# RWKV stage of a hybrid decoder step on one Trainium2 core: diagonal blocks stored to scratch by DMA from the product tile, five PSUM copies and an affine step on another engine

## The chip, the core and the metric

One core of one Trainium2 chip: TensorE (PE in the profile) with its weight loads (PEld), VectorE (DVE), ScalarE (ACT), GpSimd (POOL), the queue of SyncE (SP), from which all DMAs of this kernel are issued, and 16 DMA engines. The metric is the time of one execution in microseconds of the device.

## The reference

One layer over 1040 prompt tokens (16 of them meta tokens) and 8 x 8 sample tokens, everything in float32: a projection of the normed input to 5896 columns, an RWKV-7 branch and an mLSTM branch, a gated merge, and an MLP. The change touches the RWKV branch alone:

```python
a = jax.nn.sigmoid(a0 + al @ a_up)
w = -jax.nn.softplus(-(w0 + jnp.tanh(wl) @ w_up)) - 0.5        # decay = exp(-exp(w))
kk = heads(k * k_k); kk = kk * lax.rsqrt(jnp.maximum(jnp.sum(kk * kk, axis=-1, keepdims=True), 1e-24))
k = k * (1.0 + (a - 1.0) * k_a)

def _rwkv7_step(S, inp):
    r, w, k, v, kk, a = inp
    sa = jnp.einsum('bhvk,bhk->bhv', S, -kk)
    S = S * w[:, :, None, :] + sa[..., None] * (kk * a)[:, :, None, :] + v[..., None] * k[:, :, None, :]
    return S, jnp.einsum('bhvk,bhk->bhv', S, r)

y = _head_norm(y, gn_g, RW_GN_EPS) + gn_b
y = y + jnp.sum(r * k * r_k, axis=-1, keepdims=True) * v
y = y.reshape(B, T, D_RW) * g
```

There are 8 heads of 64. The scan over tokens is computed in chunks of 64 tokens, where the step above becomes matrix products and the inverse of a unit triangular 64x64 matrix.

## The kernel before

The RWKV part runs 24 passes: `j` counts 4 pairs of heads (two heads lie on the halves of the 128 partitions, `HP`), `g` counts 6 groups of `G` = 3 chunks; the last group (`g` = 5) also holds the 64 sample tokens. Each pass has four stages, written as generators that yield between their pieces: `stage_a` prepares the operands of a group and makes `X1`; `stage_b` of the group before inverts the triangular matrices; `stage_c` of the one before that carries the state; `stage_d` norms the output. `ORDER` says in which order the pieces of the four stages follow each other, and how many matmuls of the big input projection (`L283`, `L285`, `L287`) are pulled in between. The order on TensorE is thus written by hand and is kept as written. On VectorE, ScalarE, GpSimd and SP a scheduler places the instructions by its own estimate of when each can run, and each engine then executes its queue in order.

The names that matter here, with the lines of the profile:

- `X1` (`L713` on TensorE, `L715` on VectorE): three products per group, scaled and masked while they leave PSUM. Columns 128 to 192 of each chunk hold the strictly lower triangular matrix to be inverted.
- `nd4`, `nd` (`L719`, `L721`): `X1` masked to its four 16x16 blocks on the diagonal, and these folded to 16 columns. `nd` goes to scratch in DRAM (`ndr`, `L723`) and comes back as `NR` (`L725`), in which each partition holds a whole 16x16 block. Both are issued on SP, the second one when the first has landed.
- The chain on `NR` (`L773`, `L775`, tiles `tmp` and `x`): 15 rounds of a product and a sum on VectorE, which invert the 16x16 blocks. `XC` and `XT` (`L777`, `L780`) are the result and its transpose.
- The rest of `stage_b` widens the inverse from 16 to 32 to 64. TensorE makes products at `L785`, `L630`, `L801`, `L808` and `L814`, and between them their results leave PSUM: `QC`, `XC` again, `QZ` (`L803`, twice), the off-diagonal part of `bd["x"]` (`bdx`, `L810`, twice) and `ATb` (`L817` on ScalarE, `L818` on VectorE).
- `stage_c`: `L827` to `L831` multiply by `ATb`; `GH` and `MR` (`L838` to `L843`) leave PSUM; then, chunk after chunk, `L901` multiplies by the state `Vs` and `L909` on VectorE scales the new state out of PSUM. The next `L901` needs it.
- `stage_d`: squares (`sqd`), a sum over each head (`head_sum`, `L621` to `L623`, in which the part lost by a rounded copy is computed by the subtraction `L622` and added in a second matmul), a reciprocal root by Newton steps (`newton`, `L174` to `L182`), and `yo` (`L967` to `L969`).

Of the kernel before, what the change touches and what calls it, by code (L numbers as in the profile page):

```python
# [8 lines left out]
F32 = mybir.dt.float32  # L9
F32R = mybir.dt.float32r  # L10
I32 = mybir.dt.int32
AF = mybir.ActivationFunctionType
ALU = mybir.AluOpType
AX = mybir.AxisListType
# [15 lines left out]
G = 3  # L30
# [72 lines left out]
def tile_hybrid_trunk_step(ctx, tc, x_prompt, x_sample, st_S, st_shift, st_C, st_n, st_m, st_conv,  # L103
# [4 lines left out]
    nc = tc.nc  # L108
# [38 lines left out]
    dma = nc.sync.dma_start  # L147
    act = nc.scalar.activation
    V = nc.vector
# [225 lines left out]
    with banks(s=4, m=2), ExitStack() as st:  # L375
# [91 lines left out]
        with tc.manual_schedule(engines={mybir.EngineType.Activation, mybir.EngineType.PE}):  # L467
# [23 lines left out]
            V.tensor_scalar(out=NKK, in0=PRM[:, P_KK:P_KK + 4], scalar1=-1.0, scalar2=None, op0=ALU.mult)  # L491
            V.tensor_scalar(out=OKA, in0=PRM[:, P_KA:P_KA + 4], scalar1=-1.0, scalar2=1.0, op0=ALU.mult, op1=ALU.add)
            ps = sbank()
# [84 lines left out]
    ATb = gp.tile([128, G, 2, 2, 64], F32, name="ATb")  # L578
    KB = gp.tile([128, G, 3, 64], F32, name="KB")
    LMS = [gp.tile([128, G, 65], F32, name=f"LM{i}") for i in range(3)]  # L580
    for t_ in LMS:
# [23 lines left out]
    def g3(ap):  # L605
        return ap.rearrange("p (c t) -> p c t", c=G)
# [12 lines left out]
    def head_sum(ps, x, hi, lo, eng):  # L619
        hr, xr = hi.bitcast(F32R), lo.bitcast(F32R)  # L620
        nc.scalar.copy(out=hr, in_=x)  # L621
        eng.tensor_tensor(out=xr, in0=x, in1=hi, op=ALU.subtract)  # L622
        return lambda: [mm(ps(), lhsT=obr, rhs=t_, start=(y == 0), stop=(y == 1)) for y, t_ in enumerate((hr, xr))]  # L623

    def tl(n, sh=(GC,), bufs=1):
        return gp.tile([128] + list(sh), F32, tag=n, name=n, bufs=bufs)
# [15 lines left out]
    def stage_a(j, g, st):  # L642
# [34 lines left out]
        yield  # L677
        V.tensor_scalar(out=wa, in0=wa, scalar1=0.5, scalar2=0.5, op0=ALU.mult, op1=ALU.add)
        tw, ta = wa[:, 0], wa[:, 1]
        cc = tl("cc")  # L680
        V.tensor_tensor_scan(out=cc, data0=K["rms" if smp else "rm"], data1=tw, initial=0.0, op0=ALU.mult, op1=ALU.add)
# [11 lines left out]
        bt = tl("bt")  # L693
        V.scalar_tensor_tensor(out=bt, in0=zk, scalar=pc(P_KK), in1=ta, op0=ALU.mult, op1=ALU.mult)
        at = tw
        V.scalar_tensor_tensor(out=g3(at), in0=g3(zk), scalar=NKK[:, j:j + 1], in1=lx, op0=ALU.mult, op1=ALU.mult)
        for h, s in enumerate(HP):
            nc.scalar.copy(out=bd["a"][s, :, h, :], in_=g3(at)[s])
        V.tensor_tensor(out=KB[:, :, 2, :], in0=g3(bt), in1=g3(li), op=ALU.mult)
        act(out=ta, in_=ta, func=AF.Identity, scale=pc(P_KA), bias=OKA[:, j:j + 1])  # L700
        V.tensor_tensor(out=ta, in0=ta, in1=zk, op=ALU.mult)
# [15 lines left out]
        st["X1"] = X1  # L717
        nd4 = tl("bt", (G, 4, 16))
        V.tensor_tensor(out=nd4.rearrange("p c b s -> p c (b s)"), in0=X1[:, :, 128:192], in1=b3(K["m16"]), op=ALU.mult)  # L719
        nd = tl("nd", (G, 16))  # L720
        V.tensor_reduce(out=nd, in_=nd4.rearrange("p c b s -> p c s b"), axis=AX.X, op=ALU.add)  # L721
        scr = ndr[j * NG + g]
        dma(out=scr, in_=nd.rearrange("p c s -> p (c s)"))  # L723
        NR = tl("NR", (16, G, 16))
# [41 lines left out]
    def stage_b(j, g, st):  # L766
# [35 lines left out]
        for i, q in enumerate(HQ):  # L802
            V.tensor_copy(out=QZ[q], in_=ps[q, :32 * G])  # L803
        yield
# [4 lines left out]
        for h, q in enumerate(HQ):  # L809
            V.tensor_copy(out=bd["x"][q, :, h, 32:], in_=ps[q, :32 * G].rearrange("p (c d) -> p c d", c=G))  # L810
        yield
# [5 lines left out]
        nc.scalar.copy(out=at[HP[0], :, 0::3], in_=pv[HP[0]])  # L817
        V.tensor_copy(out=at[HP[1], :, 1:3], in_=pv[HP[1]])  # L818
        yield
# [123 lines left out]
    def stage_d(j, g, st):  # L943
# [11 lines left out]
        sv = sq[:, c0:].rearrange("p c t -> p (c t)")  # L955
        sr = head_sum(lambda: pv_[:, :ny], sv, tl("nt")[:, :ny], tl("yo")[:, :ny], PO)
        yield
# [904 lines left out]
```

## Time and profile before

| | us |
|---|---|
| three runs, median | 2055.19 |
| three runs, lowest and highest | 2053.84, 2058.42 |
| the profiled execution | 2053.6 |
| its span, from first to last instruction | 2051.8 |
| TensorE busy in the span | 1943.2 |
| VectorE busy in the span | 1266.4 |
| ScalarE busy in the span | 729.1 |
| GpSimd busy in the span | 589.4 |

The profile is of one execution. Busy times are unions of the instructions' times; matmuls overlap each other, so that a matmul row of 0.35 us may start 0.19 us behind the one before it. The RWKV passes run from about 95 to 830 us; the mLSTM branch, the merge and the MLP follow.

### The profile page before, as it was taken

The numbers are of one execution on the slowest core, as the hardware profiler recorded it, in microseconds if no ns is written. First come the engines' busy times: TensorE is split into PE (matmuls) and PEld (weight loads), VectorE is DVE, ScalarE is ACT, GpSimd is POOL, SyncE is SP. The second block draws the span as 40 slices with busy tenths as digits, with TensorE's granted clock in tenths as the row PEclk, the third lists the DMA queues.
The fourth block names the chain that finished last, engine by engine and source line by source line (L and its number), as shares of the span: only waits on it lengthen the run. The fifth ranks groups of instructions, "written<-read, shape, count | busy, mean of one in ns | idle before, by whom it ended". The sixth has DMA issues, their size and how long they took to land.

```text
span 2051.8 us, 32757 instructions
## 1 busy us (share of the span) xinstructions
PE 1943.2 (95%) x12325; PEld 1762.7 (86%) x12325; DVE 1266.4 (62%) x3527; ACT 729.1 (36%) x1706; POOL 589.4 (29%) x937
## 2 busy tenths in 40 slices
PE   8999899999999999999899998999999999999996
PEld 8988788888888888989788777889999999988895
DVE  6378778867877887777765469244444444444447
ACT  6444344433443343546554234322222222211122
POOL 3321221322122121353435115133222322232225
PEclk9999999999999999999999999999999999999998
DMA  5222112112111221143756334111111111111114
GB/s 157 56 77 66 47 56 64 58 47 67 63 56 56 67 66 57 54 129 117 233 185 206 132 99 153 32 52 42 52 52 42 42 51 43 42 42 52 42 37 163
DMA packets 148495, 161.63 MB, mean 79 GB/s; under 512 B 20428, under 2 KB 121606, under 8 KB 148336
## 3 DMA queue, kind: packets, MB, share of 16 engines
q1 hardware_dynamic: 148336, 159.54, 24.6%
q8 instruction: 97, 1.59, 0.3%
q14 instruction: 62, 0.51, 0.1%
HBM read 121.98 MB, written 37.27 MB: 78 GB/s over the span
## 4 chain that ended last, share of the span: by engine, by line
PE 63%; DVE 22%; DMA 7%; issue 3%; ACT 2%; POOL 1%; SPq 0%; DVEq 0%; ACTq 0%; POOLq 0%
PE g L219 11%; PE g L221 11%; PE g L220 11%; PE g L287 5%; PE g L283 5%; PE g L285 5%; DMA NR<-ndr 3%; DVE tmp L773 2%; DVE x L775 2%; DMA ndr<-nd 1%; PE g L1735 1%; DVE Vs L909 1%; PE a L713 1%; PE g L1635 1%; PE g L1637 1%
## 5 line engine op out<-in xcount | busy, mean ns | idle before, releaser
L207 POOL TENSOR_TENSOR lo<-raw,hi 128x128 fp32r<-128x128 f32 (+1 forms) x736 | 414.7, 596 | 985.8 <-ACT hi L200 971.6
L283 PE MATMUL g<-u,hi 128*128 128x414 f32 (+4 forms) x1120 | 379.8, 339 | 1.5 <-ACT hi L200 0.8
L287 PE MATMUL g<-u,lo 128*128 128x414 f32 (+4 forms) x1120 | 381.0, 340 | 0.0
L285 PE MATMUL g<-u,hi 128*128 128x414 f32 (+4 forms) x1120 | 378.9, 338 | 0.0
L200 ACT CAST hi<-raw 128x1024 fp32r<-128x1024 f32 x124 | 128.6, 1048 | 379.3 <-PE g L1735 275.8
L219 PE MATMUL g<-mg,hi 128*128 128x384 f32 (+1 forms) x768 | 251.7, 328 | 0.6 <-ACT mg L1609 0.6
L220 PE MATMUL g<-mg,hi 128*128 128x384 f32 (+1 forms) x768 | 251.4, 327 | 0.3 <-DVE mg L1610 0.3
L221 PE MATMUL g<-mg,lo 128*128 128x384 f32 (+1 forms) x768 | 251.5, 328 | 0.0
L1771 DVE TENSOR_TENSOR ACC<-g,ACC 128x512 f32<-128x512 f32 x234 | 161.4, 690 | 129.5 <-PE g L221 123.4
L283 PEld LDWEIGHTS g<-u,hi 128*128 128x128 f32 x1120 | 214.1, 191 | 6.8 <-issue 1.5
L287 PEld LDWEIGHTS g<-u,lo 128*128 128x128 f32 x1120 | 213.8, 191 | 4.9 <-POOL lo L207 0.3
L285 PEld LDWEIGHTS g<-u,hi 128*128 128x128 f32 x1120 | 213.7, 191 | 3.7 <-issue 0.2
L219 PE MATMUL g<-hi,ah 128*128 128x512 f32 (+1 forms) x515 | 202.9, 394 | 0.0
L220 PE MATMUL g<-lo,ah 128*128 128x512 f32 (+1 forms) x515 | 202.7, 394 | 0.0
L221 PE MATMUL g<-hi,ah 128*128 128x512 f32 (+1 forms) x515 | 202.4, 393 | 0.0
L219 PEld LDWEIGHTS g<-mg,hi 128*128 128x128 f32 x768 | 144.1, 188 | 1.5 <-ACT mg L1609 0.9
L220 PEld LDWEIGHTS g<-mg,hi 128*128 128x128 f32 x768 | 144.2, 188 | 1.2 <-DVE mg L1610 0.5
L221 PEld LDWEIGHTS g<-mg,lo 128*128 128x128 f32 x768 | 144.2, 188 | 0.0
L221 PEld LDWEIGHTS g<-hi,ah 128*128 128x128 f32 x515 | 96.7, 188 | 22.9
L219 PEld LDWEIGHTS g<-hi,ah 128*128 128x128 f32 x515 | 96.6, 187 | 22.3
L220 PEld LDWEIGHTS g<-lo,ah 128*128 128x128 f32 x515 | 96.7, 188 | 22.0
L773 DVE TENSOR_TENSOR tmp<-NR,x 128x45 f32<-128x45 f32 (+4 forms) x360 | 82.5, 229 | 28.4 <-DMA NR<-ndr 21.1
(855 smaller groups left out, 3482.1 us busy)
## 6 DMA issues: line engine op xcount, KB each, us to landing
raw<-in_w_in_dram SPq DMA_DIRECT2D x44, 512.0 KB
raw<-in_w_ff_up_dram SPq DMA_DIRECT2D x32, 512.0 KB
raw<-in_w_ff_down_dram SPq DMA_DIRECT2D x32, 512.0 KB
NR<-ndr SPq DMA_DIRECT2D x24, 384.0 KB
gscr<-gst SPq DMA_DIRECT2D x16, 544.0 KB
xt<-in_x_prompt_dram SPq DMA_DIRECT2D x15, 512.0 KB
ga<-gscr SPq DMA_DIRECT2D x8, 544.0 KB
pscr<-ga SPq DMA_DIRECT2D x8, 544.0 KB
```

Of the source, the lines that this page charges most:

```text
L200: nc.scalar.copy(out=hi, in_=raw)
L207: PO.tensor_tensor(out=lo[:, k:k + step], in0=raw[:, k:k + step], in1=hi[:, k:k + step].bitcast(F32), op=ALU.subtract)
L219: mm(ps, lhsT=wh, rhs=xh, start=(i == 0), stop=False)
L220: mm(ps, lhsT=wh, rhs=xl, start=False, stop=False)
L221: mm(ps, lhsT=wl, rhs=xh, start=False, stop=(i == last))
L283: mm(ps, lhsT=hi[:, k], rhs=xh, start=(k == 0), stop=False)
L285: mm(ps, lhsT=hi[:, k], rhs=xl, start=False, stop=False)
L287: mm(ps, lhsT=lo[:, k], rhs=xh, start=False, stop=(k == 7))
L713: mm(ps[:, 192 * (c - c0):192 * (c - c0) + 192], lhsT=flat(bd["a"][:, c]), rhs=flat(KB[:, c]), start=True, stop=True)
L773: V.tensor_tensor(out=tmp[:, :, :n], in0=NR[:, s + 1:16, :, s].rearrange("p t c -> p c t"), in1=x[:, :, s:s + 1].broadcast_to([128, G, n]) ...
L775: V.tensor_tensor(out=x[:, :, s + 1:16], in0=x[:, :, s + 1:16], in1=tmp[:, :, :n], op=ALU.add)
L1771: V.tensor_tensor(out=ACC[:, i, cs], in0=ps, in1=ACC[:, i, cs], op=ALU.add)
```

## The change

The diagonal blocks go from `X1` to scratch by eight DMAs, one for each 16 partitions (16 partitions x 3 chunks x 16 numbers); `nd4`, `nd` and their two instructions are gone. The two `QZ` copies, the two `bdx` copies and the second half of `ATb` are issued on ScalarE. The step from tanh to sigmoid is no longer one VectorE instruction over both halves of `wa`: the `w` half is done on ScalarE, and for the `a` half 0.5 is folded into the constants (`OKA`, `PRH`) and 1.0 is added in `bt`; the factor `k_k` moves into the second `KB` product. The subtraction in `head_sum` for `sqd` runs on VectorE, where GpSimd had it.

```diff
-            V.tensor_scalar(out=OKA, in0=PRM[:, P_KA:P_KA + 4], scalar1=-1.0, scalar2=1.0, op0=ALU.mult, op1=ALU.add)
+            V.tensor_scalar(out=OKA, in0=PRM[:, P_KA:P_KA + 4], scalar1=-0.5, scalar2=1.0, op0=ALU.mult, op1=ALU.add)
...
-        V.tensor_scalar(out=wa, in0=wa, scalar1=0.5, scalar2=0.5, op0=ALU.mult, op1=ALU.add)
         tw, ta = wa[:, 0], wa[:, 1]
+        act(out=tw, in_=tw, func=AF.Identity, scale=0.5, bias=half)
...
-        V.scalar_tensor_tensor(out=bt, in0=zk, scalar=pc(P_KK), in1=ta, op0=ALU.mult, op1=ALU.mult)
+        V.scalar_tensor_tensor(out=bt, in0=ta, scalar=1.0, in1=zk, op0=ALU.add, op1=ALU.mult)
...
-        V.tensor_tensor(out=KB[:, :, 2, :], in0=g3(bt), in1=g3(li), op=ALU.mult)
-        act(out=ta, in_=ta, func=AF.Identity, scale=pc(P_KA), bias=OKA[:, j:j + 1])
+        V.scalar_tensor_tensor(out=KB[:, :, 2, :], in0=g3(bt), scalar=PRH[:, P_KK + j:P_KK + j + 1], in1=g3(li), op0=ALU.mult, op1=ALU.mult)
+        act(out=ta, in_=ta, func=AF.Identity, scale=PRH[:, P_KA + j:P_KA + j + 1], bias=OKA[:, j:j + 1])
...
-        nd4 = tl("bt", (G, 4, 16))
-        V.tensor_tensor(out=nd4.rearrange("p c b s -> p c (b s)"), in0=X1[:, :, 128:192], in1=b3(K["m16"]), op=ALU.mult)
-        nd = tl("nd", (G, 16))
-        V.tensor_reduce(out=nd, in_=nd4.rearrange("p c b s -> p c s b"), axis=AX.X, op=ALU.add)
         scr = ndr[j * NG + g]
-        dma(out=scr, in_=nd.rearrange("p c s -> p (c s)"))
+        for r in range(0, 128, 16):
+            dma(out=scr[r:r + 16].rearrange("p (c s) -> p c s", c=G), in_=X1[r:r + 16, :, 128 + r % 64:144 + r % 64])
...
-            V.tensor_copy(out=QZ[q], in_=ps[q, :32 * G])
+            nc.scalar.copy(out=QZ[q], in_=ps[q, :32 * G])
...
-            V.tensor_copy(out=bd["x"][q, :, h, 32:], in_=ps[q, :32 * G].rearrange("p (c d) -> p c d", c=G))
+            nc.scalar.copy(out=bd["x"][q, :, h, 32:], in_=ps[q, :32 * G].rearrange("p (c d) -> p c d", c=G))
...
-        V.tensor_copy(out=at[HP[1], :, 1:3], in_=pv[HP[1]])
+        nc.scalar.copy(out=at[HP[1], :, 1:3], in_=pv[HP[1]])
...
-        sr = head_sum(lambda: pv_[:, :ny], sv, tl("nt")[:, :ny], tl("yo")[:, :ny], PO)
+        sr = head_sum(lambda: pv_[:, :ny], sv, tl("nt")[:, :ny], tl("yo")[:, :ny], V)
```

The order on TensorE is the same in both programs, and on SP the eight DMAs stand where the one stood, with `NR` right behind them. The scheduler's order on VectorE changes. Three places show it; lines of the changed program are one or two off those of before (`L772` and `L774` are the chain).

On VectorE in the pass `j` = 2, `g` = 2, from the row ahead of the chain's first product on (`128x3x15`), before:

```order
L174 SCALAR_TENSOR_TENSOR nt<-nt 128x192
L773 TENSOR_TENSOR tmp<-NR,x 128x3x15
L174 SCALAR_TENSOR_TENSOR dg<-nt,dg 128x192
L818 COPY ATb<-b 64x3x128
L967 SCALAR_TENSOR_TENSOR yo<-ys,PRM,dg 128x192
L775 TENSOR_TENSOR x<-x,tmp 128x3x15
L968 SCALAR_TENSOR_TENSOR yo<-yo,PRM,bv 128x192
L773 TENSOR_TENSOR tmp<-NR,x 128x3x14
L756 TENSOR_TENSOR bv<-a,Zv 128x192
L969 TENSOR_TENSOR yo<-yo,gg 128x192
L775 TENSOR_TENSOR x<-x,tmp 128x3x14
L838 TENSOR_TENSOR GH<-s,Ct 64x3x64 x2
```

The same stretch in the changed program, up to the first round of the chain:

```order
L636 TENSOR_TENSOR MB<-a,Ct 128x3x64
L174 SCALAR_TENSOR_TENSOR nt<-nt 128x192
L174 SCALAR_TENSOR_TENSOR dg<-nt,dg 128x192
L966 SCALAR_TENSOR_TENSOR yo<-ys,PRM,dg 128x192
L967 SCALAR_TENSOR_TENSOR yo<-yo,PRM,bv 128x192
L968 TENSOR_TENSOR yo<-yo,gg 128x192
L755 TENSOR_TENSOR bv<-a,Zv 128x192
L837 TENSOR_TENSOR GH<-s,Ct 64x3x64 x2
L841 TENSOR_TENSOR MR<-s,RB_764 64x3x64 x2
L772 TENSOR_TENSOR tmp<-NR,x 128x3x15
L774 TENSOR_TENSOR x<-x,tmp 128x3x15
```

`dg`, the three `yo`, `bv`, `GH` and the first `MR` pair now stand ahead of the chain, where they stood behind its first product; `ATb` is gone from the queue.

On VectorE in a pass with sample tokens (`j` = 2, `g` = 5), around the same product, before:

```order
L803 COPY QZ<-b 32x96 x2
L773 TENSOR_TENSOR tmp<-NR,x 128x3x15
L775 TENSOR_TENSOR x<-x,tmp 128x3x15
L961 TENSOR_SCALAR sqd<-c 128x192
L773 TENSOR_TENSOR tmp<-NR,x 128x3x14
L176 TENSOR_SCALAR dg<-sqd 128x192
L775 TENSOR_TENSOR x<-x,tmp 128x3x14
L174 SCALAR_TENSOR_TENSOR nt<-dg 128x192
L810 COPY bdx<-b 32x3x32 x2
L179 TENSOR_TENSOR nt<-nt,sqd 128x192
L773 TENSOR_TENSOR tmp<-NR,x 128x3x13
L174 SCALAR_TENSOR_TENSOR dg<-nt,dg 128x192
```

and in the changed program:

```order
L793 STREAM_TRANSPOSE XT<-XC 128x192
L960 TENSOR_SCALAR sqd<-c 128x192
L176 TENSOR_SCALAR dg<-sqd 128x192
L174 SCALAR_TENSOR_TENSOR nt<-dg 128x192
L179 TENSOR_TENSOR nt<-nt,sqd 128x192
L174 SCALAR_TENSOR_TENSOR dg<-nt,dg 128x192
L174 SCALAR_TENSOR_TENSOR nt<-dg 128x192
L182 TENSOR_TENSOR nt<-nt,sqd 128x192
L772 TENSOR_TENSOR tmp<-NR,x 128x3x15
L174 SCALAR_TENSOR_TENSOR nt<-nt 128x192
L774 TENSOR_TENSOR x<-x,tmp 128x3x15
L174 SCALAR_TENSOR_TENSOR dg<-nt,dg 128x192
```

The rows from `sqd` to the fourth Newton product (seven rows) have moved ahead of the chain's first product, and the `QZ` and `bdx` copies are gone.

On VectorE in the pass behind it (`j` = 3, `g` = 0), from the chain's first product on, before; the first pair of `Vs` rows is the fifth row after the last one shown:

```order
L773 TENSOR_TENSOR tmp<-NR,x 128x3x15
L775 TENSOR_TENSOR x<-x,tmp 128x3x15
L773 TENSOR_TENSOR tmp<-NR,x 128x3x14
L843 TENSOR_TENSOR MR<-s,Ct 64x2x64 x2
L775 TENSOR_TENSOR x<-x,tmp 128x3x14
L663 TENSOR_SCALAR rho<-a 64x2
L848 TENSOR_TENSOR mq<-s,Ct 128x64
L664 TENSOR_SCALAR rho<-a 64x1
L663 TENSOR_SCALAR rho<-a 64x2
L664 TENSOR_SCALAR rho<-a 64x1
L773 TENSOR_TENSOR tmp<-NR,x 128x3x13
L665 RECIPROCAL rho<-rho 128x3
```

and in the changed program, up to that pair:

```order
L842 TENSOR_TENSOR MR<-s,Ct 64x2x64 x2
L665 TENSOR_SCALAR rho<-a 64x2
L847 TENSOR_TENSOR mq<-s,Ct 128x64
L666 TENSOR_SCALAR rho<-a 64x1
L665 TENSOR_SCALAR rho<-a 64x2
L666 TENSOR_SCALAR rho<-a 64x1
L667 RECIPROCAL rho<-rho 128x3
L772 TENSOR_TENSOR tmp<-NR,x 128x3x15
L774 TENSOR_TENSOR x<-x,tmp 128x3x15
L772 TENSOR_TENSOR tmp<-NR,x 128x3x14
L774 TENSOR_TENSOR x<-x,tmp 128x3x14
L908 TENSOR_SCALAR Vs<-c,LM_759 64x65 x2
```

The second `MR` pair, `rho` and `mq` have moved ahead of the chain, and `Vs` follows after two rounds instead of four and a half.

## Rows read from the trace of the kernel before

**Rows 1.** The page, its first part: the span, and the busy time of TensorE with its share of the span and its instructions.

```profile
span 2051.8 us, 32757 instructions
...
PE 1943.2 (95%) x12325; PEld 1762.7 (86%) x12325; DVE 1266.4 (62%) x3527; ACT 729.1 (36%) x1706; POOL 589.4 (29%) x937
```

**Rows 2.** Busy time of each engine (us, and instructions) in two stretches, 95 to 830 us and the rest to the end, with the granted clock, the DMA share and GB/s.

```profile
95.00:830.00 735.00, 679.74 (x5462) 622.33 (x5461) 570.01 (x2120) 292.35 (x795) 158.32 (x322) 0.98 0.20 60
830.00:2051.00 1221.00, 1174.87 (x6303) 1055.59 (x6301) 647.43 (x1295) 382.55 (x796) 396.08 (x534) 0.99 0.27 87
```

**Rows 3.** The waits of 95 to 830 us: engine and line that waited, what it waited for, us in total, times, longest us.

```profile
PE c L901 <- DVE Vs L909: 39.3, 38, 2.8
...
DVE tmp L773 <- DMA NR<-ndr: 21.1, 11, 4.2
...
PE b L814 <- DVE bdx L810: 4.6, 3, 1.7
```

**Rows 4.** TensorE in order of time in one pass, 510.5 to 537 us: start, us, engine, line, operation, written tile <- read tiles, form, count; in brackets the idle time before it and what ended that.

```profile
511.10 0.54 PE L785 MATMUL b<-XC,X 64*64 64x32 f32 x12
...
517.78 0.83 PE L814 MATMUL b<-X,bdx 128*128 128x128 f32 x6
...
520.72 0.83 PE L827 MATMUL s<-MB,ATb 128*128 128x128 f32 x6
...
529.21 0.34 PE L901 MATMUL c<-Vs,GH 128*64 128x65 f32 x4 [1.71 <-DVE Vs L909]
...
532.71 0.34 PE L901 MATMUL c<-Vs,GH 128*64 128x65 f32 x4 [0.61 <-DVE Vs L909]
...
536.44 0.54 PE L785 MATMUL b<-XC,X 64*64 64x32 f32 x12
```

**Rows 5.** VectorE in the same pass, the same columns.

```profile
510.89 1.07 DVE L715 SCALAR_TENSOR_TENSOR X<-a,rho,Ct 128x192 f32<-128x192 f32 x3 [1.71 <-PE a L713]
...
512.42 0.49 DVE L721 TENSOR_REDUCE nd<-bt 128x48 f32<-128x192 f32 x1
...
514.80 0.51 DVE L803 COPY QZ<-b 32x96 f32<-32x96 f32 x2 [0.47 <-PE b L801]
...
519.42 0.23 DVE L773 TENSOR_TENSOR tmp<-NR,x 128x45 f32<-128x45 f32 x1
519.57 0.34 DVE L174 SCALAR_TENSOR_TENSOR dg<-nt,dg 128x192 f32<-128x192 f32 x1
519.95 0.56 DVE L818 COPY ATb<-b 64x384 f32<-64x384 f32 x1
520.54 0.42 DVE L967 SCALAR_TENSOR_TENSOR yo<-ys,PRM,dg 128x192 f32<-128x192 f32 x1
...
521.26 0.64 DVE L968 SCALAR_TENSOR_TENSOR yo<-yo,PRM,bv 128x192 f32<-128x192 f32 x1
...
522.31 0.36 DVE L756 TENSOR_TENSOR bv<-a,Zv 128x192 f32<-128x192 f32 x1
522.58 0.35 DVE L969 TENSOR_TENSOR yo<-yo,gg 128x192 f32<-128x192 f32 x1
...
523.23 0.73 DVE L838 TENSOR_TENSOR GH<-s,Ct 64x192 f32<-64x192 f32 x2
524.00 0.72 DVE L842 TENSOR_TENSOR MR<-s,RB 64x192 f32<-64x192 f32 x2
...
529.30 0.35 DVE L678 TENSOR_SCALAR wa<-wa 128x384 f32<-128x384 f32 x1
...
535.59 0.36 DVE L777 TENSOR_TENSOR XC<-x,Ct 128x192 f32<-128x192 f32 x1
```

**Rows 6.** The SP queue in order of time in two stretches, 206 to 209 us and 512.8 to 515.2 us: start, us for which the queue is held (where there is a count, for all of them), line, written <- read.

```profile
206.54 1.13 SPq L518 DMA_DIRECT2D wur<-in_rw_w_up_dram  x2
207.71 1.24 SPq L518 DMA_DIRECT2D wur<-in_rw_a_up_dram  x2
...
512.93 0.32 SPq L723 DMA_DIRECT2D ndr<-nd  x1
514.45 0.61 SPq L725 DMA_DIRECT2D NR<-ndr  x1
```

**Rows 7.** Groups of instructions by line and form in 95 to 830 us: line, engine, operation, written <- read, form, count, then busy us and mean ns of one, then idle time before them and what ended it.

```profile
L810 DVE COPY bdx<-b 32x96 f32<-32x96 f32 x48 | 11.9, 249 | 2.7 <-PE b L808 1.7 <-issue 0.2
...
L817 ACT COPY ATb<-b 64x384 f32<-64x384 f32 x24 | 11.3, 472 | 7.9 <-PE b L814 7.8
L622 POOL TENSOR_TENSOR yo<-sqd,nt 128x192 fp32r<-128x192 f32 x19 | 11.3, 595 | 26.9 <-ACT nt L621 14.4 <-DMA yscr<-yo 7.0 <-DVE X L715 3.1
...
L739 ACT COPY Vs<-a 64x65 f32<-64x65 f32 x48 | 9.9, 207 | 0.6
...
L719 DVE TENSOR_TENSOR bt<-X,Ct 128x192 f32<-128x192 f32 x24 | 9.0, 373 | 0.1
```

**Rows 8.** The chain that ended last, in order of time, 408 to 419 us: start, us, what.

```profile
407.70 1.07 DVE X L715 x3
...
409.78 3.42 DMA ndr<-nd
...
413.22 5.40 DMA NR<-ndr
...
418.65 0.24 DVE tmp L773
```

More of the change, by code (lines that the diff above doesn't have):

```diff
@@ L579, in tile_hybrid_trunk_step @@
     KB = gp.tile([128, G, 3, 64], F32, name="KB")
+    half = gp.tile([128, 1], F32, name="half")
+    V.memset(half, 0.5)
     LMS = [gp.tile([128, G, 65], F32, name=f"LM{i}") for i in range(3)]
```

## The prediction

> **What bounds the kernel now.** The page comes first: TensorE is busy 95% of the span and carries most of the chain that ended last [rows 1]. So an edit on VectorE can only give back time in which TensorE stands still. The windows say where that is: the RWKV part, 95 to 830 us, holds 735 - 680 = 55 us of idle TensorE and a VectorE that is busy 570 us of 735; behind it the touched code no longer runs [rows 2]. 55 us, 2.7%, is the ceiling. The waits then say what TensorE stands still for: 39 us for `Vs`, the scaled PSUM evacuation on VectorE, in 38 waits of up to 2.8 us, and 4.6 us for `bdx`; VectorE in turn waits 21 us, in 11 of 24 passes, for `NR`, which comes back through DRAM [rows 3].
>
> To see what ends last, walk one pass (j = 2, g = 2, 511 to 536 us) on both engines. TensorE starts `L785` at 511.10 and again at 536.44: the period is 25.34 us. It reaches `L827` at 520.72, 9.62 us later, without a wait; its idle time, 1.71 + 0.61, comes behind that, at the two `Vs` waits [rows 4]. VectorE makes `X1` at 510.89 to 511.96, first uses `NR` at 519.42, starts `GH` at 523.23, about 1.6 us after `L827` has made it possible (520.72 + 0.83 of matmuls = 521.6 at the earliest), and ends with `XC` at 535.59, on which the next `L785` rests [rows 4, 5]. From `GH` on, VectorE runs almost back to back. It is late there, `Vs` sits in the same queue, and so TensorE waits.
>
> **What the change takes and adds, per pass.** VectorE loses the mask product and the reduction (0.37 + 0.49), four small copies (4 x 0.25), the large copy (0.56) and the affine step (0.35) [rows 5, 7]: 2.8 us. It gains the subtraction, 0.36 as the `bv` row, a plain product of the same 128x192, has it [rows 5]; a scalar added to the second `KB` product is below 0.1. Net about -2.4 us in each of 24 passes, 57 us in all if every one of them lay on the path.
>
> ScalarE gains the copies: a 64x65 copy takes 0.21 there and the sister copy of `ATb` 0.47 [rows 7], so 4 x 0.22 + 0.47 + some 0.36 = 1.7 us per pass. It is busy 292 of 735 us [rows 2], so I price this at nothing. The cover is thin at one place: `L814` at 517.78 needs `bdx` [rows 4], and on ScalarE four `Vs` copies now stand ahead of it. Without the cover it costs up to 0.3 us a pass, 7 us in all, on the stretch to `L827`. GpSimd loses 0.6 us [rows 7] for which nobody waits.
>
> **The transfer.** Before, `NR`'s second transfer is issued at 514.45, that is 2.49 us after `X1` ends: 0.97 for mask and reduction, then 1.52 from issue to landing of one DMA, of which the issue holds the queue 0.32 [rows 5, 6]. Now eight DMAs must be issued one after the other, and all must land. Their issue price is in no row. Below: 0.32 each, as the one they replace. Above: the four `wur` loads, also of a part of the partitions, take 1.13 + 1.24 = 2.37 us, 0.60 each, and `NR`'s own issue 0.61 [rows 6]. I take 0.60, since these transfers are like those pieces of a tensor rather than a whole one. Then the last issue ends 8 x 0.60 = 4.8 us after `X1`, it lands as long after its issue as before (1.52 - 0.32 = 1.2, say 1.2 to 1.5), and `NR` is issued at 6.0 to 6.3 instead of 2.49: 3.6 later. By the low price it would be 8 x 0.32 + 1.2 = 3.8, 1.3 later. With 5.0 for `NR` itself (514.45 to 519.42 [rows 5, 6]) the first `tmp` can start 11.2 us after `X1`, where it was 7.5.
>
> The Trainium skill, page "DMA: Bandwidth & Descriptors", Specifications, asks for at least 512 bytes per piece, below which the engine does a read-modify-write; the new pieces have 64. The old ones had 192 and the whole transfer was through in 1.52 us [rows 6], so no such penalty shows in the rows; doubling a transfer of this size would move the sum by some tenths of a microsecond at most, and I leave it out.
>
> **Where the pass then ends.** The order of the instructions, the first pair of order rows above, decides it: in the new program `GH` and `MR` stand ahead of the first `tmp`. So `tmp` starts at the later of two times, counted from `L785`. By `NR`: `X1` ends at 0.86 and `NR` is there at 0.86 + 11.2 = 12.1. By `GH`: `L827` at 9.62, `GH` at 10.5, `GH` and `MR` 1.45: 12.0. They meet, which is why I see no large gain and no large loss here. What remains behind `tmp` was 16.17 us (519.42 to 535.59). Of it go, to ScalarE or ahead of the wait, `dg` 0.34, `ATb` 0.56, three `yo` (0.42, 0.64, 0.35), `bv` 0.36, `GH` 0.73, `MR` 0.72 and the affine step 0.35: 4.5 us; the subtraction's 0.36 comes [rows 5]. That leaves 12.1. With `XC`'s 0.36 and 0.1 to the matmul the period is 12.1 + 12.1 + 0.5 = 24.7 against 25.34: 0.6 us. The `Vs` waits shrink by about 1.5 us, but a wait of `L785` for `XC` takes most of their place.
>
> Named by `j` and `g`, seven passes are of this kind (g = 2 and 3, but for the very first): 7 x 0.6 = 4.2 us. Three long ones (g = 5, j < 3) have the scratch transfer stuck, behind a weight load: 3.42 us, and `tmp` 9.9 us after `X1` [rows 8]. There the eight issues run while the first one waits anyway, so `NR` comes 1.9 later (4.8 + 1.5 + 5.4 = 11.7); but behind `tmp` two `bdx` copies and `ATb` (1.1) go, seven rows of the Newton steps (about 2.4, at 0.35 each) move ahead of the wait, and 0.36 comes: -3.1. Gain 1.2 each, 3.5 us together; TensorE's wait for `bdx` [rows 3], which was queued behind this wait, goes with it. The three passes after them (g = 0, j > 0) have `Vs` close behind the `NR` wait, the 2.8 us of [rows 3]: `NR` comes 2 to 3.6 later, but five rows of the chain, one `MR` pair and six short rows no longer stand between (some 0.22, 0.6 and 0.17 each, as such rows take): -2.7. About 0. In six passes (g = 4 and g = 1, without first and last) a long run of matmuls lies behind `XC`, and only their `Vs` wait shortens, by 0.25 as I estimate from the two limits: 1.5 us. The first two and the last two passes, where less leaves the tail, lose 1 together by the same two limits (an estimate). Sum: 4.2 + 3.5 + 0 + 1.5 - 1 = 8 us. The profiled execution took 2053.6, so 2045.6 by its own account; it was 1.6 below the median of the three runs, 2055.19, which gives **2047 us**.
>
> **Rivals.** (1) *All of the relief arrives*: issues at 0.32, `NR` 2.3 earlier than I take it, and a tail 0.6 shorter than its rows add up to. Then the seven gain 1.2 each, the long three 2.5, the three after them 1.3, the six 1.0: 8.4 + 7.5 + 3.9 + 6 + 1 = 27, half of the 55 us: 2028. For it: VectorE runs back to back when TensorE waits [rows 4, 5]. Against: two limits meet at 12 us, and the issue price moves only one of them. (2) *`NR` is late* (slower). Each microsecond beyond 11.2 costs that much in the some 17 passes in which `tmp` waits for `NR`: 8/17 = 0.5 us eats the gain, that is an issue price of 0.66; at 0.75 per issue, or a landing 1.2 us longer, it is 17 x 1.2 - 8 = 12 us slower: 2067. For it: `NR`'s own issue at 0.61, and the queue also carries the weight loads. Against: four issues in 2.37 us. (3) *The eight pay one by one*: each issue waits for the landing before it, 8 x 1.52 = 12.2 us before `NR` can be issued, 9.7 later than now, of which some 5 us reach the period: 24 x 5 = 120 us, 2175. The `wur` rows speak against it, with four issues in 2.4 us [rows 6]. The Trainium skill, page "DMA: Bandwidth & Descriptors", Rules for kernel authors, says of two transfers to disjoint partition halves that they serialize and that splitting is not worth it; by that rule the time would go this way. (4) *ScalarE's copies stand in the way*: 0.3 to 0.5 us in each pass before `L827`, which eats the 8 us: no change. (5) *Nothing moves*, since removed waits only change their name: 2055.
>
> **How the numbers follow.** A measurement here tells 0.2%, 4 us. Chances: forecast, 2040 to 2051, 35%; rival 1, 14%; rivals 4 and 5, 22%; rival 2, 26%; rival 3, 3%. Faster is the first two, 49%; same 22%; slower 29%. The range takes in most of rivals 1 and 2: 2028 to 2069.
>
> **What would show it.** SP: eight issues per pass, 0.6 apart (0.32: rival 1). `tmp` about 11 us behind `X1`, with waits for `NR` in more passes than 11, together some 30 us instead of 21. TensorE's waits for `Vs` down from 39 to below 20 us, new ones of `L785` for `XC`, about 1 us each. VectorE some 57 us less busy, ScalarE 40 us more, TensorE's idle time in 95 to 830 us at 47. Waits of `L808`, `L814` or `L827` for ScalarE would be rival 4. The prediction is wrong if the eight issues cost other than 0.5 to 0.66 each, or if VectorE stands idle behind `tmp`.

## The result and the profile after

The changed kernel takes **2082.2 us** (median of four runs, 2079.0 to 2084.2) where the kernel before, run beside it, takes 2056.8: a ratio of 1.0119, 95% interval 1.0092 to 1.0146. It is 25 us slower; 8 us faster had been forecast, and the range ended at 2069. The profiled execution took 2083.5. The page, first the span and then busy time and share of each engine:

```profile
span 2081.7 us, 32856 instructions
PE 1963.2 (94%) x12325; PEld 1782.0 (86%) x12325; DVE 1206.7 (58%) x3360; ACT 773.7 (37%) x1850; POOL 570.6 (27%) x913
```

The work moved as intended: VectorE is 60 us less busy than before, ScalarE 45 us more. But TensorE, with the same 12325 instructions in the same order, is busy 1963.2 us instead of 1943.2 [rows 1]: the same matmuls ran slower. The windows of the RWKV part and of what follows (length, busy time and instructions of each engine, the granted clock, the share and the rate of the DMA engines):

```profile
95.00:860.00 765.00, 700.00 (x5464) 641.86 (x5463) 507.70 (x1950) 337.01 (x938) 144.56 (x302) 0.95 0.21 58
860.00:2081.00 1221.00, 1174.25 (x6294) 1054.95 (x6292) 649.58 (x1296) 382.24 (x796) 391.03 (x529) 0.99 0.27 87
```

The second row has the 1221 us that the stretch behind the RWKV part had before [rows 2]; the 30 us lie in the first, and its clock fell from 0.98 to 0.95. Two accounts say how much each is. TensorE's idle time is the span less its busy time: 2051.8 - 1943.2 = 108.6 before, 118.5 now, 10 us more. Time lost to the clock is the span by what is missing of the mean granted clock, 0.987 before and 0.975 now: 26.7 and 52.0, 25 us more. (Together 35 for 30, since part of a slow stretch can lie in idle time.) These are two single executions, and the one of the kernel before had a higher clock than most: over 80 executions of that kernel the clock loss averages 34.4 us, and over the four of the changed kernel 49.4 us, which makes 15 of the 24 us between their mean times. **So by either account most of the loss is a slower TensorE, and the waits themselves are the smaller part.**

The waits of the same stretch (total, times, longest, in us) against [rows 3]:

```profile
DVE tmp L772 <- DMA NR<-ndr: 51.9, 24, 3.8
PE c L900 <- DVE Vs L908: 46.4, 35, 3.8
PE b L784 <- DVE XC L776: 10.8, 10, 5.5
```

All 24 passes now wait for `NR`, TensorE's waits for `Vs` grew instead of shrinking, and the longest single ones are 3.8 and 5.5 us, where 2.8 was the longest for `Vs`. What one does is seen in the pass j = 1, g = 0, first on VectorE, then on TensorE (start, duration, shape, in brackets idle time before and who ended it):

```profile
286.51 0.18 DVE L667 RECIPROCAL rho<-rho 128x3 f32<-128x3 f32 x1
290.29 0.23 DVE L772 TENSOR_TENSOR tmp<-NR,x 128x45 f32<-128x45 f32 x1 [3.61 <-DMA NR<-ndr]
...
291.17 0.58 DVE L908 TENSOR_SCALAR Vs<-c,LM 64x65 f32<-64x65 f32 x2
```

```profile
287.75 0.34 PE L285 MATMUL g<-u,hi 128*128 128x398 f32 x1
291.80 0.49 PE L900 MATMUL c<-Vs,GH 128*64 128x65 f32 x4 [3.72 <-DVE Vs L908]
...
292.93 0.53 PE L283 MATMUL g<-u,hi 128*128 128x398 f32 x1
```

```profile
284.00:288.00 4.00, 4.00 (x28) 3.59 (x27) 1.86 (x10) 2.26 (x7) 3.21 (x8) 1.00 0.46 122
288.00:291.80 3.80, 0.09 (x1) 0.00 (x0) 1.36 (x7) 0.00 (x0) 0.00 (x0) 0.94 0.85 244
291.80:305.00 13.20, 13.20 (x56) 11.74 (x56) 6.73 (x30) 4.45 (x12) 1.16 (x2) 0.50 0.02 6
305.00:309.00 4.00, 4.00 (x32) 3.70 (x33) 3.50 (x15) 0.00 (x0) 0.62 (x1) 1.00 0.15 33
```

VectorE has nothing left that stands ahead of `tmp` and waits 3.61 us. `Vs`, whose matmul has long been done, stands four rows behind `tmp` in the same queue, so TensorE waits 3.72 us for it. Behind the wait the granted clock is 0.50, that is 1.2 GHz, for all 13.2 us that the third window shows, with TensorE busy all the time and a matmul on 398 columns at 0.53 us. Half of 13.2 is lost on top of the wait. Along the whole RWKV part the trace has 72 us at 1.2 GHz, 24 before; 13 of the 17 TensorE waits of 1.5 us or more have such a stretch beginning in them or within 2 us behind them. This is no rule: in the kernel before it holds for 2 of 8 such waits, and in the run e1 below for 2 of 10.

### The profile page after: what moved, and what is told of

It reads as the page before. It is cut to its first block, busy times and chain, and to the rows that moved or that the text cites. A ratio compares the mean times of both kernels' runs of the same rounds, so it can differ in the third digit from the quotient of the medians.

```text
span 2081.7 us, 32856 instructions
## 1 busy us (share of the span) xinstructions
PE 1963.2 (94%) x12325; PEld 1782.0 (86%) x12325; DVE 1206.7 (58%) x3360; ACT 773.7 (37%) x1850; POOL 570.6 (27%) x913
## 5 line engine op out<-in xcount | busy, mean ns | idle before, releaser
L207 POOL TENSOR_TENSOR lo<-raw,hi 128x128 fp32r<-128x128 f32 (+1 forms) x736 | 409.9, 592 | 1045.4 <-ACT hi L200 1028.1
L287 PE MATMUL g<-u,lo 128*128 128x414 f32 (+4 forms) x1120 | 387.2, 346 | 0.0
L283 PE MATMUL g<-u,hi 128*128 128x414 f32 (+4 forms) x1120 | 385.9, 345 | 0.8 <-ACT hi L200 0.8
L285 PE MATMUL g<-u,hi 128*128 128x414 f32 (+4 forms) x1120 | 384.4, 343 | 0.0
L283 PEld LDWEIGHTS g<-u,hi 128*128 128x128 f32 x1120 | 218.6, 195 | 6.2 <-issue 1.5
L287 PEld LDWEIGHTS g<-u,lo 128*128 128x128 f32 x1120 | 218.0, 195 | 5.4 <-POOL lo L207 0.3
L285 PEld LDWEIGHTS g<-u,hi 128*128 128x128 f32 x1120 | 218.4, 195 | 4.0 <-issue 0.2
L219 PEld LDWEIGHTS g<-hi,ah 128*128 128x128 f32 x515 | 96.6, 187 | 22.3
L772 DVE TENSOR_TENSOR tmp<-NR,x 128x45 f32<-128x45 f32 (+4 forms) x360 | 74.5, 207 | 59.6 <-DMA NR<-ndr 51.9
```

The source lines that it names most:

```text
L207: PO.tensor_tensor(out=lo[:, k:k + step], in0=raw[:, k:k + step], in1=hi[:, k:k + step].bitcast(F32), op=ALU.subtract)
L219: mm(ps, lhsT=wh, rhs=xh, start=(i == 0), stop=False)
L283: mm(ps, lhsT=hi[:, k], rhs=xh, start=(k == 0), stop=False)
L285: mm(ps, lhsT=hi[:, k], rhs=xl, start=False, stop=False)
L287: mm(ps, lhsT=lo[:, k], rhs=xh, start=False, stop=(k == 7))
L772: V.tensor_tensor(out=tmp[:, :, :n], in0=NR[:, s + 1:16, :, s].rearrange("p t c -> p c t"), in1=x[:, :, s:s + 1].broadcast_to([128, G, n]) ...
```

## The experiments

All times are medians; idle and clock loss come from each profiled execution as above, and the last column is the clock loss as the mean over all executions of a kernel, since one execution can lie far from it (e6 was profiled in its slowest execution, e17 in its fastest). The first `tmp` is given as its start less the end of `X1`, mean of the 24 passes. "Masked" is the changed kernel with mask, reduction and single DMA put back; "order" says where `tmp` was tied in VectorE's queue. e4, e7 and e13 leave diagonal blocks out and take other columns in their place (e4 six of eight, e7 and e13 four of eight): they tell what a transfer costs and compute something else.

| kernel | us | ratio to before, 95% | tmp behind X1 | idle | clock loss | clock loss, all |
|---|---|---|---|---|---|---|
| before | 2056.8 | | 8.2 | 108.6 | 26.7 | 34.4 |
| changed | 2082.2 | 1.009 to 1.015 | 12.1 | 118.5 | 52.0 | 49.4 |
| e1 masked | 2042.0 | 0.990 to 0.995 | 8.1 | 100.1 | 28.6 | 31.9 |
| e2 before + eight DMAs | 2093.3 | 1.014 to 1.020 | 12.3 | 132.2 | 48.1 | 48.1 |
| e3 issues on SP and ScalarE | 2078.8 | 1.008 to 1.011 | 10.1 | 121.7 | 35.2 | 38.9 |
| e4 one DMA | 2054.5 | 0.997 to 1.000 | 7.4 | 103.7 | 28.7 | 33.9 |
| e5 masked, GpSimd subtracts | 2045.5 | 0.993 to 0.997 | 7.9 | 97.7 | 30.6 | 31.7 |
| e6 masked + a hop | 2051.2 | 0.995 to 0.998 | 10.4 | 99.7 | 43.1 | 36.5 |
| e7 four DMAs | 2067.4 | 1.003 to 1.007 | 9.4 | 110.4 | 41.3 | 43.4 |
| e8 before + five copies | 2055.2 | 0.996 to 1.000 | 8.1 | 107.3 | 28.7 | 33.5 |
| e9 changed, order in g = 0 | 2070.8 | 1.004 to 1.008 | 12.1 | 114.1 | 45.6 | 38.8 |
| e10 masked, order in g = 0 | 2037.9 | 0.987 to 0.991 | 8.1 | 94.2 | 26.5 | 29.0 |
| e11 before + affine, subtraction | 2053.6 | 0.996 to 0.999 | 8.0 | 101.4 | 34.9 | 33.7 |
| e12 issues on SP and GpSimd | 2074.6 | 1.005 to 1.011 | 9.6 | 118.5 | 45.6 | 45.1 |
| e13 four DMAs, order | 2032.0 | 0.986 to 0.990 | 11.9 | 92.5 | 22.3 | 23.9 |
| e14 masked, order | 2030.5 | 0.985 to 0.990 | 11.6 | 90.1 | 24.4 | 24.3 |
| e15 = e10 + held Vs | 2070.4 | 1.004 to 1.009 | 8.0 | 113.9 | 47.6 | 47.1 |
| e16 changed, order | 2062.7 | 1.001 to 1.005 | 13.4 | 113.0 | 32.9 | 32.0 |
| e17 before, order | 2043.3 | 0.991 to 0.996 | 11.6 | 94.9 | 24.4 | 29.3 |

**Which part of the change costs.** e1 undoes the transfer and keeps the rest; e2 makes the transfer alone.

```diff
 # e1, in the changed kernel (e2 is the reverse, in the kernel before)
+        V.tensor_tensor(out=nd4..., in0=X1[:, :, 128:192], in1=b3(K["m16"]), op=ALU.mult)
+        V.tensor_reduce(out=nd, in_=nd4..., axis=AX.X, op=ALU.add)
-        for r in range(0, 128, 16):
-            dma(out=scr[r:r + 16]..., in_=X1[r:r + 16, :, 128 + r % 64:144 + r % 64])
+        dma(out=scr, in_=nd.rearrange("p c s -> p (c s)"))
```

> The changed kernel with the mask product, the reduction and the single DMA put back; the copies on ScalarE, the affine step and the subtraction on VectorE stay as changed. Theory 1 (the eight issues make NR late, so that TensorE's single waits for Vs grow to 2 to 4 us, and the stretches at 1.2 GHz follow them): the first tmp comes about 8 us behind X1 again instead of 12.1, TensorE's stretches at 1.2 GHz in the RWKV part add up to 25 us or less instead of 72, and the time is 2035 to 2050. Theory 2 (the moved copies and the moved subtraction cost the time themselves): 2070 to 2082, with as many stretches at 1.2 GHz as in the changed kernel. Theory 3 (the pieces of 64 bytes are slow in flight, not their issues): as theory 1 here.

> The kernel before with the eight DMAs in place of mask product, reduction and single DMA, and nothing else changed. Theory 1: NR is as late as in the changed kernel (tmp 12 us behind X1) and VectorE has 1.5 us per pass more to do behind it, so the time is at or above that of the changed kernel, 2082 to 2105. Theory 2: 2050 to 2060, as before. Theory 3: as theory 1.

Both came out as theory 1 had it. Without the eight DMAs the other edits make the kernel 0.8% faster than before, 16 us; alone the DMAs cost 35 us. Theory 2 falls. Which of the other edits carries it, three runs ask: e5 puts the subtraction back on GpSimd in e1, e8 moves the five copies alone, e11 the affine step and the subtraction alone.

> The kernel with the mask and the single DMA put back (2042), and the subtraction back on GpSimd as well: only the five copies and the affine step are moved. Theory 1 (VectorE is late behind the wait for NR, so what leaves that stretch shortens TensorE's waits for Vs): VectorE has 0.36 us per pass less, 0.2 to 0.4 us of it shows in most passes, 2034 to 2042. Rival: the subtraction lies in VectorE's idle time at the wait for NR (34 us there), and the result is the same as with it on VectorE, 2040 to 2044.

> The kernel before with the five copies moved to ScalarE and nothing else. Theory 1: most of what leaves VectorE behind the wait for NR is in these copies (1.6 of 1.9 us per pass), so most of the gain of 15 us comes with them: 2041 to 2048. Rival (the gain comes from the affine step ahead of the scan, which makes the chain to X1 shorter): 2052 to 2058.

> The kernel before with the affine step on ScalarE and the subtraction on VectorE, the five copies back on VectorE and the mask and single DMA as before. With the five copies and the affine step the time was 2045, with all three 2042, with the copies alone 2055, before 2057. If the gains of the parts add up, the affine step and the subtraction carry it: 2043 to 2048. If it takes the copies and the affine step together (each alone leaves the same rows late): 2052 to 2057.

By the ratios the copies alone give 5 us, the affine step and the subtraction 6, copies and affine step 10, all three 16. Theory 1 of e5 and of e8 missed, and e11 came out by its second reading: no part carries the gain alone. Whether the parts simply add up (5 and 6 against 16) and whether the subtraction's place matters (2042.0 against 2045.5) is within the intervals.

**What about the transfer costs.** Half the issues on another queue (e3 ScalarE, e12 GpSimd), half as many issues (e7), one (e4), or a late `NR` without any of it (e6).

```diff
-            dma(out=scr[r:r + 16]...
+            (dma if r % 32 else nc.scalar.dma_start)(out=scr[r:r + 16]...      # e3; PO in e12
 # e7: range(0, 128, 32), scr[r:r + 32], X1[r:r + 32]    e4: dma(out=scr..., in_=X1[:, :, 128:144])
 # e6, in e1:
+        dma(out=hop, in_=nd...); dma(out=scr, in_=hop)
```

> The changed kernel with the eight DMAs issued in turn from SP and from ScalarE, four each. Theory 1: the last issue ends about 2.5 us behind X1 instead of 5, so tmp comes 9.5 to 10 us behind X1, and half or more of the loss goes: 2050 to 2066, less what ScalarE's own work loses by 2.5 us of issues per pass. Theory 2: 2080 or above, since ScalarE has more to do. Theory 3: the transfers land as late as before, tmp at 11.5 to 12, 2078 to 2085.

> The changed kernel with the eight DMAs issued in turn from SP and from GpSimd, four each: like the run with SP and ScalarE, without ScalarE's queue standing behind four issues in each pass (17 us of TensorE's waits there were for QZ and Vs from ScalarE). Theory 1: tmp 9.5 to 10.5 us behind X1 and no waits of TensorE for QZ or for Vs from ScalarE, 2055 to 2066, as with four DMAs. Rival (issuing from two queues costs as much as it saves, since GpSimd's issues are slower than SP's): tmp 11.5 us or more behind X1, 2075 to 2085.

> The changed kernel with one DMA that takes columns 128 to 144 of every row of X1, so that seven in eight... of the diagonal blocks is left out: only the first block of each half is the right one, the others are other columns. Pieces of 64 bytes as in the changed kernel, 384 of them, but one issue, and neither mask nor reduction on VectorE. Theory 1: NR is issued some 2 us behind X1, tmp starts as soon as VectorE is there, 2025 to 2045, the fastest of the four. Theory 2: 2070 to 2082. Theory 3: tmp stays over 11 us behind X1, 2070 to 2085.

> The changed kernel with four DMAs of 32 rows each instead of eight of 16; every second diagonal block is left out (other columns of X1 stand in its place). The same number of pieces of 64 bytes, half the issues. Theory 1: the last issue ends 2.5 us earlier, tmp 9.6 to 10 us behind X1, 2052 to 2068. Rival (the pieces in flight, not the issues, make the transfer long): tmp 11.5 us or more behind X1, 2075 to 2083.

> The kernel with the mask and the single DMA put back (2042), but with one more transfer, from scratch to a second scratch, between them and NR: no eight issues, no other change, only a later NR. By the rows of one DMA, 1.5 to 2 us later, so tmp 9.7 to 10.3 us behind X1. Theory 1 (the lateness of NR itself costs, by longer single waits of TensorE for Vs and the stretches at 1.2 GHz after them): 2052 to 2072, and more than 30 us of stretches at 1.2 GHz. Rival (the eight issues or their pieces cost in another way, on SP's queue or in the DMA engines): 2040 to 2047.

In the four runs with other issues (e3, e12, e4, e7) the first `tmp` came about as early as theory 1 said (10.1, 9.6, 7.4, 9.4 us), so theory 3 falls: the issues make the length, and the pieces in flight hardly do. But the times don't follow. Of the four, e7 alone lies in the range of theory 1, at its upper end. e4, with the earliest `NR` and the least on VectorE, was to be the fastest and is 12 us behind e1. e3 has a cause of its own. Rows of ScalarE in one pass, where `ACTq` is its queue of issues, and two rows of TensorE's waits:

```profile
361.68 2.50 ACTq L722 DMA_DIRECT2D ndr<-X  x4
364.23 0.72 ACT L795 COPY bdx<-XC 64x192 f32<-64x192 f32 x2 [2.09 <-DMA ndr<-X]
364.98 0.47 ACT L802 COPY QZ<-b 32x96 f32<-32x96 f32 x2
...
PE b L807 <- ACT QZ L802: 8.7, 13, 1.8
PE a L752 <- ACT Vs L738: 8.3, 4, 2.8
```

The four issues hold ScalarE for 2.5 us, its copies follow behind them, and TensorE waits 17 us for `QZ` and `Vs` from there, where the changed kernel has 0.2. e12, without that, is still 16 us slower than before, though GpSimd's issues took no longer than SP's (0.53 against 0.59 us), as its rival had it; and e6, with the later `NR`, is 16 us faster than e7. Lateness does cost: with `tmp` 2.3 us later than in e1, e6 is 9 us slower, just under the range of its theory 1. But e7, only 1.3 us later than e1, is 25 us slower. So the lateness of `NR` is not the whole price. The waits of e6, then of e7:

```profile
PE c L906 <- DVE Vs L914: 32.6, 36, 3.1
DVE tmp L778 <- DMA NR<-ndr: 30.6, 19, 3.0
```

```profile
PE c L900 <- DVE Vs L908: 44.4, 35, 3.5
DVE tmp L772 <- DMA NR<-ndr: 37.3, 20, 4.8
```

With the later `NR`, VectorE waits less for it, and so does TensorE for `Vs`. The two programs differ in VectorE's order, though not in it alone: in the passes g = 3, j > 0, 19 rows of the timeline stand between the first `tmp` and the next `Vs` in e6, 27 in e7, 35 in e4, 31 in e1 and 15 in the changed kernel. The count by itself does not put the times in order, so it is a hint and no more. The new theory: **what costs is what stands in VectorE's queue behind the row that waits for `NR`.** e4 was not tried with another order, and why it is behind e1 stays open.

**The order alone.** e9 and e10 tie the first `tmp` behind the first `Vs` pair in the three passes g = 0, j > 0; e13, e14, e16 and e17 also tie it behind the last `MR` row in the passes g = 1 to 4. Nothing else in the program changes; the scheduler places the other rows anew.

```diff
         for s in range(15):
-            V.tensor_tensor(out=tmp[:, :, :n], ...)
+            with tc.issue_after(vst["ins"]) if s == 0 and (0 < g < 5 or g == 0 and j) and "ins" in vst else ExitStack():
+                V.tensor_tensor(out=tmp[:, :, :n], ...)
 # vst["ins"] is the last MR row, in the pass g = 5 of stage_c the first Vs pair (e9, e10: that one alone, and the condition is g == 0 and j)
```

> The changed kernel with one constraint more and nothing else: in the three passes g = 0, j > 0 VectorE's first tmp (which waits there for NR for 3.3 to 3.8 us) is queued behind the first Vs pair instead of ahead of it. NR is as late as before, the eight issues are the same. Theory 1 (the wait for NR costs because Vs is queued behind it; TensorE's waits of 3.4 to 3.8 us there, and the 31 us at 1.2 GHz that follow them, are its price): these three waits fall below 1 us and most of the stretches after them go; 3 x 2.7 us of waits and up to 31/2 us of clock, so 2058 to 2072. Rival (the lateness of NR costs through XC, or through the issues on SP's queue): 2077 to 2083, no change.

> The same constraint in the kernel with mask product, reduction and single DMA put back (2042), where TensorE waits 2.2, 1.9 and 2.3 us for Vs in these three passes. Theory 1: these waits fall below 1 us, 4 us of waits and 3 to 8 us of clock go: 2031 to 2039. Rival (the first tmp, and with it XC, comes later by as much as Vs comes earlier): 2040 to 2045.

> The kernel with four DMAs of 32 rows (every second diagonal block left out; 2067), with its first tmp held in VectorE's queue behind the last MR row in the passes g = 1 to 4, and behind the first Vs pair in the passes g = 0, j > 0; nothing else changed, NR as late as it was there. Theory 1a (the wait for NR costs by the rows that stand behind it in VectorE's queue: GH, MR and Vs): TensorE's waits for Vs fall from 44 to 25 to 33 us, and the time to 2045 to 2058, although NR comes no earlier. Rival (what costs is the lateness of XC, which NR's arrival sets): 2063 to 2070, since XC comes no earlier.

> The same constraints in the kernel with mask product, reduction and single DMA put back (2042; with the constraint in the passes g = 0 alone 2038). Here NR comes early, 7 to 8 us behind X1, so the constraint in the passes g = 1 to 4 makes the first tmp wait for GH and MR instead of the other way round. Theory 1a: waits for Vs fall by some 5 us more, waits for XC grow in the passes g = 2 and 3, which have 1.6 to 2.7 us of room there: 2030 to 2040. Rival (the chain of tmp to XC is the tighter one once NR is early): 2040 to 2050.

> The changed kernel, all eight DMAs, with the first tmp held behind the last MR row in the passes g = 1 to 4 and behind the first Vs pair in the passes g = 0, j > 0. GH and MR already stand ahead of tmp in most of these passes, but in g = 1 and g = 4 some 20 to 30 rows of other work stood between tmp and Vs. By the four DMAs (tmp at 11.4 to 11.7 behind X1 with no wait, by the constraint alone; here NR arrives at 11.2 to 13.2): theory 1a: waits for Vs fall from 46 to 15 to 25 us, the stretches at 1.2 GHz from 72 to 30 or less, 2036 to 2052, faster than before. Rival (with eight issues NR itself is too late in most passes, whatever the order): 2058 to 2072.

> The kernel before with the same constraints and nothing else: mask, reduction, single DMA, the copies and the affine step on VectorE and the subtraction on GpSimd as they were. If the order is worth as much without the moved rows (12 us from 2042 to 2030 with them), 2040 to 2048; if the moved rows were what made room for it, 2050 to 2058; if the order alone is what was to be had, 2028 to 2036.

All but e16 came out by this theory, e13 beyond it. Three rows of 360 tied are worth 11 us in e9 and 4 in e10. The gain lies where the theory puts it. From one product of `XC` (`L785`) to the next, the three tied passes of e9 are 12.7 us shorter together and the other 21 together 1.0 longer; in e17 the passes g = 0 and 4, j > 0, win 11.7, where VectorE waited for `NR` in five of six, and those with g = 1 to 3, where one of nine waited, 1.3. e13 is the clearest: `NR` as in e7, `tmp` later, and 35 us faster. Its waits:

```profile
PE b L785 <- DVE XC L777: 19.2, 17, 2.7
DVE tmp L773 <- DMA NR<-ndr: 12.8, 5, 4.4
PE c L902 <- DVE Vs L910: 9.9, 22, 0.9
```

The waits for `Vs` fell from 44.4 to 9.9 us, none over 0.9; part of them returned as waits for `XC`, in small pieces of about 1 us, and the clock loss halved. The same order makes the best kernel, e14, 2030.5. But e16 missed: with all eight DMAs the order wins 19 us and leaves the kernel still slower than before. Its waits:

```profile
DVE tmp L773 <- DMA NR<-ndr: 27.0, 14, 3.5
PE c L902 <- DVE Vs L910: 24.9, 31, 2.4
PE b L785 <- DVE XC L777: 22.9, 20, 5.3
```

In the tied passes g = 2 and 3 the queue lets `tmp` start 11.4 to 11.7 us behind `X1` (e14, no wait); with eight DMAs it started there at 11.9 to 13.2 (j > 0), after waits for `NR` of up to 1.5 us, and that reaches `XC`: the three passes g = 2 became 4.0 us longer together by the tie. So both hold: the order is worth 19 us (e16), and beyond that the last four of the eight issues cost 31 (e16 against e13), as with them `NR` comes later than the order can cover. That VectorE is spared the mask shows no gain once the order is right (2032.0 in e13, 2030.5 in e14).

**The clock.** e15 holds up the first `Vs` pair in the four passes g = 3 of the stage that makes it, where nothing but TensorE's next matmul waits.

```diff
+                        if c == 0 and g == 3:
...
+                            V.tensor_scalar(out=hold[s], in0=pS[s, :64], scalar1=lc[s], scalar2=None, op0=ALU.mult)
+                            for _ in range(6):
+                                V.tensor_copy(out=hold[s], in_=hold[s])
+                            vl = V.tensor_copy(out=Vn[s, cn, h, :64], in_=hold[s])
...
```

> The fastest kernel so far (2038), with the first Vs pair of the four passes g = 3 of the stage that makes it held up: each half goes through six more copies of itself on VectorE, 14 rows or some 2.5 us in all. XC has 10 us of room in the step where this falls, so the only thing lost is the wait of TensorE for Vs, four times 2.5 us, 10 us in all. Theory 1b (single waits of TensorE of 3 us and more are followed by stretches at 1.2 GHz): four new stretches of 3.4 to 13.7 us follow them, 14 to 40 us more at 1.2 GHz, of which half is lost: 2055 to 2068. Rival (the clock goes by something else): no stretches at these places, 2046 to 2050.

The waits became longer than meant (3.8 to 6.0 us, and a second one of 2.7 to 3.4 us behind each), and the time came out 2 us beyond theory 1b's range. The windows ahead of and behind the first and the third:

```profile
199.00:210.00 11.00, 8.99 (x56) 8.41 (x54) 10.19 (x46) 2.94 (x8) 3.93 (x8) 1.00 0.29 80
212.00:222.00 10.00, 7.21 (x32) 6.83 (x33) 3.28 (x16) 1.60 (x5) 0.14 (x1) 0.53 0.00 0
...
576.00:586.00 10.00, 7.34 (x44) 6.78 (x42) 9.27 (x45) 3.00 (x8) 1.24 (x3) 1.00 0.20 57
588.00:597.00 9.00, 6.33 (x29) 5.99 (x30) 3.19 (x16) 1.79 (x5) 0.00 (x0) 0.50 0.00 0
```

Full clock ahead, 1.2 GHz from the wait on, all four times, for 6.8 to 10.2 us; e10 has no such stretch at any of the four places. Against e10, idle time grew by 20 us and the clock loss by 21 (18 over all executions), for 32 us of time; the two overlap in part. That waits as long as these bring the clock down is shown; that every long wait does is not: in the changed kernel 4 of the 17 waits of 1.5 us and more have no stretch behind them, in e1 8 of 10, and a few short stretches have no such wait in front. What decides for waits of 1.5 to 2.8 us stays open. The Trainium skill, page "TensorE: Matmul & The Clock Gate", Why this matters for your kernels, asks to keep idle gaps out between bursts of matmuls for this reason; e15 agrees.

## Why the prediction was wrong

Three steps failed: one pass was taken for all in the time of `NR`, an idle VectorE with `Vs` behind it was not priced, and TensorE's clock was in no term. The measured 2082.2 lies beyond the range and on the other side of the time before.

- **The eight issues** were priced right: 0.59 us each, 0.63 apart, the last landing 1.2 to 1.45 us after its issue (once 2.8). In the pass that was walked, j = 2, g = 2, the rows are those of the forecast:

```profile
532.41 5.04 SPq L722 DMA_DIRECT2D ndr<-X  x8
538.69 0.63 SPq L724 DMA_DIRECT2D NR<-ndr  x1
```

  The first `tmp` came 11.21 us behind `X1` (forecast 11.2) and the period was 24.60 (24.7). **One pass was taken for all.** In 10 others one of the eight issues took 1.0 to 1.4 us and all eight 5.6 to 6.2, and `NR` itself took 4.6 to 6.1, not 5.0. The mean is 12.1, up to 13.4. The seven steady passes, forecast to gain 4.2, lost 5.8: those with g = 3, j > 0 went from 24.9 or 25.1 to between 26.4 and 27.1.
- **The passes g = 0, j > 0**, forecast at "about 0", became 11.4 us longer together. `tmp` came 3.6 to 5.5 us later there, where 2 to 3.6 was reckoned with. The rows that had moved ahead of it were through long before, so VectorE stood still for 3.3 to 3.8 us with `Vs` queued behind, and TensorE waited 3.4 to 3.8 us. The stretches at 1.2 GHz in these three passes grew from 13.7 to 30.7 us. The prediction had seen that `Vs` stands there and did not price what an idle VectorE does to it; e9, which takes `Vs` out from behind the wait, wins back 11 us.
- **The passes g = 4 and g = 1**, forecast to gain 1.5, lost some 10 although `XC` had up to 8 us of room there: waits for `Vs` of 1.6 to 2.3 us, and 3.4 us at 1.2 GHz in five of the six.
- **The four passes at the ends** (j = 0, g = 1 and 2; j = 3, g = 4 and 5), forecast to lose 1 together, lost 5.5.
- **The clock** was in no term. The sum rests on the sentence that an edit on VectorE can only give back time in which TensorE stands still; but TensorE's busy time itself rose by 20 us for the same matmuls. The clock is 25 of the 30 us between the two profiles, 15 of 24 over all executions. [Rows 2] had 0.98 for the RWKV part, and that was the place to ask what lowers it.
- **Right**: the three passes g = 5 gained (6.1 us, forecast 3.5); VectorE and ScalarE moved by 60 and 45 us (57 and 40); ScalarE's copies don't stand in the way (`L826` waits 1.3 us for `ATb`, `L807` 0.2 for `QZ`), so rival 4 falls. Without the transfer the other edits win 16 us (e1), twice the gain that was forecast for all of them together. The pass that was walked came out by its mechanism, and it is one of the 13 with neither a long issue nor a late landing.
- **The rivals.** Rival 2 had the right sign and cause, but its price, 1 us per pass and microsecond, gives 17 x 0.9 - 8 = 7 us for the measured 12.1, where 25 were lost; and the loss does not go by lateness alone (e6 and e7 against e1: 9 us for 2.3 us, 25 for 1.3). Rival 3 falls: eight issues in 5.0 us and one landing of 1.3 behind them. By the rule of the Trainium skill, page "DMA: Bandwidth & Descriptors", Rules for kernel authors, the pieces would have serialized; the trace does not show that here, though its advice, not to split, would have been right by 40 us (the changed kernel against e1).

## What to carry to other kernels

When a change makes an input late, look in the waiting engine's queue for what stands behind the row that waits, and tie that row behind the work others need; here three tied rows won 11 us (e9) and 4 (e10), and all ties together 11 to 35. Price a TensorE wait together with the granted clock in the window behind it, and prefer many waits of under 1 us to few of 3. Work a sum out on the worst pass too, and not only on the one that is easy to read.

## What the hardware showed that was not expected

- A single wait of 3.72 us was followed by 13.2 us at 1.2 GHz in which TensorE was busy all the time; four added waits of 3.8 to 6.0 us, each with a second one behind it, cost 20 us of idle time and 21 us of clock (e15).
- One DMA of all 128 rows whose source is three pieces of 64 bytes per row took 0.57 us to issue (e4), as long as one of 16 rows (0.59); from one piece of 192 bytes per row it was 0.32 [rows 6]. The price went by the form and not by the size.
- Four issues on ScalarE's queue held its copies back for 2.5 us in a pass (e3).
- Single issues of 1.0 to 1.4 us occurred in 10 of 24 passes; what holds them was not tried. The DMA engines were no busier during these eight issues than during those of most other passes (share 0.05).
